# A weight-block sum of the fast-multiplication chains made by an adding transfer instead of by VectorE

## The chip, the core and the metric

The kernel runs on one core of one Trainium2 chip. The metric is the device time of the whole launch in microseconds; of the kernel before, three runs were timed. All names of lines are those of the profile: L687 is line 687 of the kernel before. TensorE is PE in the profile, VectorE DVE, ScalarE ACT, GpSimd POOL, SyncE SP.

## The reference

One layer of a diffusion trunk, on 1024 latent tokens and 256 context tokens of width 1024, all in float32. The change touches the two feed-forwards, their first two weight matrices only:

```
def swiglu(h, w1, w3, w2):
    return (jax.nn.silu(h @ w1) * (h @ w3)) @ w2
...
x = x + 0.5 * m_l[2] * swiglu(modulate(rms_norm(x, norm1_w), m_l[0], m_l[1]), ffn1_w1, ffn1_w3, ffn1_w2)
...
x = x + 0.5 * m_l[8] * swiglu(modulate(rms_norm(x, norm3_w), m_l[6], m_l[7]), ffn2_w1, ffn2_w3, ffn2_w2)
```

`w1` and `w3` are 1024 x 2816, `w2` is 2816 x 1024. Between the feed-forwards stand retention and gated linear attention; the output is the normed latent stream.

## The kernel before, in words

**Arithmetic.** Every float32 operand is split into a high part (`hi`, the value rounded to the matmul's type, made by ScalarE, L421) and a low part (`lo`, the rest, made by VectorE, L422); a product is three matmuls, hi x hi, hi x lo and lo x hi (L426 to L428).

**Chains.** Two columns of 128 of the hidden layer and two groups of 512 tokens form a 2 x 2 block product over 8 tiles of the inner dimension, and `chain` computes it with seven half products instead of eight, after Strassen and Winograd. `seven_w` prepares the seven weight tiles of a chain, each 128 x 512. It loads four blocks from DRAM (`a11`, `a21`, `a22`, `a12`) into tiles called `raw`, and makes the other three from them on VectorE: L687 `s1 = a21 + a22`, L689 `a21 = a11 - a21`, L690 `a11 = s1 - a11`, L694 `a12 = a12 - a11`. In the order of use the seven tiles are `a11`, `s1`, the new `a11`, `a12`, the new `a21`, the new `a12`, `a22`; each is split into `whi` and `wlo` and used in 12 matmuls of 512 columns. `hidden` runs one chain for `w1` (its outputs go through SiLU) and one for `w3` (multiplied into them) per pair of hidden columns: 9 pairs in the first feed-forward, 10 in the second, so 38 chains. The first columns of each feed-forward are computed the plain way by `first1` and `first2`.

**Buffers.** There are six `raw` tiles (`NR`) for the five that a chain uses and for other weights; a load of a later chain waits until an earlier tile's last reader is done. There are six `whi` and six `wlo` tiles (`NH`).

**Beside the chains.** In the first feed-forward VectorE also computes the modulation columns (`mod_sum`, L523, one per loaded `ada` tile); in both it combines the half products (L715, L743, L751) and makes the sums for `w2` (L796, L798). The loads and the stores of the results (`gd`, `sd`) all go through SyncE's one queue (L663 is the load of a `raw` tile), in which each entry waits for its own tile. GpSimd issues no transfer at all; it computes the small power step of the norms (`nr`, L1665 and, in the second half, L147), and in the context part the low parts of some weights.

**Order.** A scheduler fixes each engine's order at build time from priorities (`WPRI` lifts a chain's preparation) and its own estimates. Around the first chain VectorE's order matters: after the norm's power step (GpSimd, `nr`) it makes four diagonal tiles (`ndiag`, L590), with which TensorE spreads the norm factors over the partitions (L599).

Of the kernel before, what the change touches and what calls it, by code (L numbers as in the profile page):

```python
# [14 lines left out]
ALU = mybir.AluOpType  # L15
# [377 lines left out]
class Trunk:  # L393
# [285 lines left out]
    def seven_w(self, w, f):  # L679
        e = self.nc.vector  # L680
        with self.tc.high_priority(offset=WPRI):
            lo, hi = slice(0, 512), slice(512, 1024)
            a11, a21, a22 = (self.raw_half(w[i][:, q]) for i, q in ((f, lo), (f + 1, lo), (f + 1, hi)))
            s1 = self.raw_half()
            a12 = self.raw_half(w[f][:, hi])
            r = [self.half(a11)]
            e.tensor_tensor(out=s1, in0=a21, in1=a22, op=ALU.add)  # L687
            r.append(self.half(s1))
            e.tensor_tensor(out=a21, in0=a11, in1=a21, op=ALU.subtract)  # L689
            e.tensor_tensor(out=a11, in0=s1, in1=a11, op=ALU.subtract)  # L690
            r.append(self.half(a11))
            r.append(self.half(a12))
            r.append(self.half(a21))
            e.tensor_tensor(out=a12, in0=a12, in1=a11, op=ALU.subtract)  # L694
            r.append(self.half(a12))
            r.append(self.half(a22))
        return r
# [1701 lines left out]
```

## Time and profile before

| | |
|---|---|
| three runs | 2085.08, 2083.58, 2084.71 us; median 2084.71 |
| profiled execution | span 2087.0 us, granted clock 0.998; no other time of it is listed |
| busy share of the span | PE 99%, PEld 84%, DVE 71%, ACT 47%, POOL 10% |
| first feed-forward's chains | about 75 to 425 us and on into the stage behind |
| second feed-forward's chains | about 1440 to 1840 us |

The span runs from the first to the last instruction of one execution. Rows of the order of time give start and duration in us, engine, line, operation, what it writes and reads, and in brackets how long the engine had been idle and what ended that. A row of SPq is the issue of a transfer, not the transfer; the time from issue to landing is listed apart.

### The profile page before, as it was taken

What the parts mean: (1) busy time and instruction counts of PE and PEld (TensorE: products, weight loads), DVE (VectorE), ACT (ScalarE), POOL (GpSimd) and SP (SyncE); (2) the same over time, 40 slices, a digit from 0 to 9 for tenths busy, and PEclk for the clock granted to TensorE, in tenths of its full rate; (3) what the DMA queues carried; (4) which work ended last, traced back from release to release, by engine and by line L of the source; (5) the groups of instructions that cost most, each with busy time, mean ns of one, the idle gap of its engine ahead of it and who ended that gap; (6) DMA issues with size and microseconds to landing.
All of it is one profiled execution on the core that took longest, in us unless ns stands there. A gap on an engine that the chain in (4) does not pass through costs nothing.

```text
span 2087.0 us, 34162 instructions
## 1 busy us (share of the span) xinstructions
PE 2071.6 (99%) x12352; PEld 1763.0 (84%) x12352; DVE 1471.9 (71%) x2660; ACT 973.3 (47%) x1818; POOL 199.3 (10%) x195
## 2 busy tenths in 40 slices
PE   9999999999999999999999999999999999999998
PEld 6888888888889999998788988888888888888888
DVE  6889999666776445765577478767776666765586
ACT  5433433435544445566475246444434344344553
POOL 0000000000015665001021001000000000010000
PEclk9999999999999999999999999999999999999999
DMA  9277667449886553674233233242344444477774
GB/s 348 84 241 237 232 217 256 149 165 371 277 289 222 181 183 115 195 219 129 76 108 98 79 91 105 90 162 81 112 156 147 144 163 157 151 235 229 218 237 151
DMA packets 201082, 370.58 MB, mean 178 GB/s; under 512 B 23249, under 2 KB 35921, under 8 KB 200785
## 3 DMA queue, kind: packets, MB, share of 16 engines
q1 hardware_dynamic: 200768, 368.33, 53.7%
q8 instruction: 97, 1.59, 0.3%
q14 instruction: 73, 0.59, 0.1%
q10 hardware_dynamic: 144, 0.07, 0.0%
HBM read 292.68 MB, written 67.24 MB: 172 GB/s over the span
## 4 chain that ended last, share of the span: by engine, by line
PE 77%; DVE 10%; DMA 8%; issue 3%; ACT 1%; SPq 0%; DVEq 0%; POOLq 0%; ACTq 0%
PE psa L147 18%; PE psa L426 10%; PE psa L428 10%; PE psa L427 10%; PE psb L147 9%; PE psb L427 7%; PE psb L428 7%; PE psb L426 7%; DVE junk L523 2%; DVE wlo L422 2%; DMA raw<-in_w 2%; DMA raw<-sd 2%; DVE hl L422 1%; DMA raw<-gd 1%; DMA hl<-sd 1%
## 5 line engine op out<-in xcount | busy, mean ns | idle before, releaser
L421 ACT ACTIVATE whi<-raw 128x512 fp32r<-128x512 f32 x371 | 233.9, 631 | 502.7 <-issue 160.6
L422 DVE TENSOR_TENSOR wlo<-raw,whi 128x512 fp32r<-128x512 f32 x371 | 254.1, 687 | 178.0 <-ACT whi L421 175.6
L426 PE MATMUL psa<-hh,whi 128*128 128x512 f32 x684 | 267.0, 390 | 1.2 <-ACT s L738 0.6
L428 PE MATMUL psa<-hh,wlo 128*128 128x512 f32 x684 | 266.3, 389 | 0.0
L427 PE MATMUL psa<-hl,whi 128*128 128x512 f32 x684 | 266.2, 389 | 0.0
L427 PE MATMUL psb<-hl,whi 128*128 128x512 f32 x568 | 221.6, 390 | 0.5 <-DVE hl L422 0.3
L428 PE MATMUL psb<-hh,wlo 128*128 128x512 f32 x568 | 221.3, 390 | 0.2 <-DVE wlo L422 0.2
L426 PE MATMUL psb<-hh,whi 128*128 128x512 f32 x568 | 221.1, 389 | 0.0
L426 PEld LDWEIGHTS psa<-hh,whi 128*128 128x128 f32 x684 | 128.4, 188 | 28.9 <-ACT s L711 1.7
L147 DVE TENSOR_TENSOR wlo<-raw,whi 128x512 fp32r<-128x512 f32 (+1 forms) x140 | 88.5, 647 | 90.8 <-ACT whi L147 80.1
L147 PE MATMUL psa<-hl,whi 128*128 128x512 f32 x384 | 152.5, 397 | 0.0
L147 PE MATMUL psa<-hh,whi 128*128 128x512 f32 x384 | 152.3, 397 | 0.0
L147 PE MATMUL psa<-hh,wlo 128*128 128x512 f32 x384 | 152.2, 396 | 0.0
L428 PEld LDWEIGHTS psa<-hh,wlo 128*128 128x128 f32 x684 | 128.4, 188 | 26.6
L427 PEld LDWEIGHTS psa<-hl,whi 128*128 128x128 f32 x684 | 128.5, 188 | 26.3
L422 POOL TENSOR_TENSOR hl<-s,hh 128x512 fp32r<-128x512 f32 x88 | 132.4, 1530 | 145.2 <-DVE hl L422 81.1
L147 ACT ACTIVATE whi<-raw 128x512 fp32r<-128x512 f32 (+1 forms) x140 | 82.5, 599 | 119.7 <-PE psa L147 94.1
L427 PEld LDWEIGHTS psb<-hl,whi 128*128 128x128 f32 x568 | 106.6, 188 | 24.7 <-DVE hl L422 2.7
L428 PEld LDWEIGHTS psb<-hh,wlo 128*128 128x128 f32 x568 | 106.6, 188 | 23.1 <-DVE wlo L422 1.2
L426 PEld LDWEIGHTS psb<-hh,whi 128*128 128x128 f32 x568 | 106.6, 188 | 22.2
L428 PE MATMUL psa<-hh,hl 128*128 128x256 f32 x392 | 111.1, 284 | 0.0
L426 PE MATMUL psa<-hh,hh 128*128 128x256 f32 x392 | 111.1, 283 | 0.0
(443 smaller groups left out, 4820.4 us busy)
## 6 DMA issues: line engine op xcount, KB each, us to landing
raw<-in_w SPq DMA_DIRECT2D x242, 256.0 KB, 3.3
s<-in_w SPq DMA_DIRECT2D x198, 256.0 KB, 3.7
gd<-s SPq DMA_DIRECT2D x154, 256.0 KB, 2.8
ada<-in_adaT SPq DMA_DIRECT2D x60, 512.0 KB, 4.6
raw<-gd SPq DMA_DIRECT2D x91, 256.0 KB, 3.5
sd<-s SPq DMA_DIRECT2D x44, 256.0 KB, 2.7
raw<-sd SPq DMA_DIRECT2D x44, 256.0 KB, 3.2
hh<-in_w SPq DMA_DIRECT2D x44, 256.0 KB, 4.0
```

The lines of the kernel that those rows point to most:

```text
L147: self.rec.add(self.eng, lambda: f(*map(get, a), **{x: get(v) for x, v in k.items()}), outs, ins, name, a, k)
L421: nc.scalar.activation(hi, src, AF.Copy)
L422: (eng or nc.vector).tensor_tensor(out=lo, in0=src, in1=hi.bitcast(F32), op=ALU.subtract)
L426: mm(ps, wa[0], xa[0], start=start, stop=False, skip_group_check=more)
L427: mm(ps, wa[0], xa[1], start=False, stop=False, skip_group_check=more)
L428: return mm(ps, wa[1], xa[0], start=False, stop=stop, skip_group_check=more)
L523: nc.vector.tensor_tensor_reduce(out=self.junk, in0=t, in1=self.cs[s], scale=1.0, scalar=self.col("ada_b")[:, j:j + 1], op0=ALU.mult, op1= ...
```

## The change

In `seven_w`, `s1` is now loaded with the block `a21` by SyncE, and GpSimd then issues a transfer of the block `a22` from DRAM that adds into `s1`. `a21` and `a22` are still loaded on their own, since both are needed later. VectorE's sum L687 is gone. The order in which the five tiles are taken changes with it: `s1`, `a11`, `a21`, `a22`, `a12`. From L684 on, every line of the changed kernel has a number higher by one; the new line 685 is the adding transfer.

```
-            a11, a21, a22 = (self.raw_half(w[i][:, q]) for i, q in ((f, lo), (f + 1, lo), (f + 1, hi)))
-            s1 = self.raw_half()
+            s1 = self.raw_half(w[f + 1][:, lo])
+            a11 = self.raw_half(w[f][:, lo])
+            self.nc.gpsimd.dma_start(s1, w[f + 1][:, hi], accum_op=ALU.add)
+            a21, a22 = (self.raw_half(w[f + 1][:, q]) for q in (lo, hi))
             a12 = self.raw_half(w[f][:, hi])
             r = [self.half(a11)]
-            e.tensor_tensor(out=s1, in0=a21, in1=a22, op=ALU.add)
             r.append(self.half(s1))
             e.tensor_tensor(out=a21, in0=a11, in1=a21, op=ALU.subtract)
```

Per chain SyncE issues five loads instead of four, GpSimd one transfer instead of none. Three places show what moves.

SyncE's queue at a chain of `w3` in the second feed-forward, before. The loads into raw_3373, 3374, 3375 and 3377 are `a11`, `a21`, `a22` and `a12` (3376 is `s1`, which is not loaded); `gd1` and `sd1` are stores of results:

```order
L663 DMA raw_3373_16610<-in_w23 128x512
L797 DMA sd1<-s_3310_16284 128x512
L799 DMA sd1<-s_3311_16285 128x512
L663 DMA raw_3374_16612<-in_w23 128x512
L752 DMA gd1<-s_3303_16194 128x512
L663 DMA raw_3375_16614<-in_w23 128x512
L752 DMA gd1<-s_3304_16208 128x512
L663 DMA raw_3377_16617<-in_w23 128x512
L752 DMA gd1<-s_3338_16439 128x512
```

The same place now; raw_3373 to raw_3377 are `s1`, `a11`, `a21`, `a22` and `a12`:

```order
L663 DMA raw_3373_16631<-in_w23 128x512
L798 DMA sd1<-s_3310_16303 128x512
L800 DMA sd1<-s_3311_16304 128x512
L663 DMA raw_3374_16633<-in_w23 128x512
L753 DMA gd1<-s_3303_16213 128x512
L663 DMA raw_3375_16636<-in_w23 128x512
L753 DMA gd1<-s_3304_16227 128x512
L663 DMA raw_3376_16638<-in_w23 128x512
L753 DMA gd1<-s_3338_16459 128x512
L663 DMA raw_3377_16640<-in_w23 128x512
```

The load of `s1` stands where that of `a11` stood, that of `a11` where that of `a21` stood, and so on; the fifth comes one store later.

VectorE's order at the end of the first norm and the start of the first chain, before. raw_224, 225, 226 and 227 are `a11`, `a21`, `a22` and `s1` of that chain:

```order
L1664 TENSOR_SCALAR nr_160_687<-psb_159_682 128x4
L1191 TENSOR_TENSOR ada4_150_612<-raw_161_693,ada3_149_611 128x512
L1191 TENSOR_TENSOR ada4_150_612<-raw_162_697,ada3_149_611 128x512
L590 TENSOR_SCALAR ndiag_163_704<-ident_4_82,nr_160_687 128x128
L590 TENSOR_SCALAR ndiag_164_706<-ident_4_82,nr_160_687 128x128
L590 TENSOR_SCALAR ndiag_165_708<-ident_4_82,nr_160_687 128x128
L590 TENSOR_SCALAR ndiag_166_710<-ident_4_82,nr_160_687 128x128
L743 TENSOR_TENSOR s_158_677<-psa_100_313,s_158_677 128x512
L687 TENSOR_TENSOR raw_227_1137<-raw_225_1133,raw_226_1135 128x512
L613 SCALAR_TENSOR_TENSOR x10_129_466<-x10_129_466,mod_7_87,nrb_170_745 128x512
L613 SCALAR_TENSOR_TENSOR x11_130_468<-x11_130_468,mod_7_87,nrb_170_745 128x512
L689 TENSOR_TENSOR raw_225_1133<-raw_224_1131,raw_225_1133 128x512
```

The same place now; raw_225 is `a11`, raw_226 is `a21`, and L690 is the line that was L689:

```order
L1665 TENSOR_SCALAR nr_160_687<-psb_159_682 128x4
L1192 TENSOR_TENSOR ada4_150_612<-raw_161_693,ada3_149_611 128x512
L1192 TENSOR_TENSOR ada4_150_612<-raw_162_697,ada3_149_611 128x512
L690 TENSOR_TENSOR raw_226_1136<-raw_225_1133,raw_226_1136 128x512
L590 TENSOR_SCALAR ndiag_163_704<-ident_4_82,nr_160_687 128x128
L590 TENSOR_SCALAR ndiag_164_706<-ident_4_82,nr_160_687 128x128
L590 TENSOR_SCALAR ndiag_165_708<-ident_4_82,nr_160_687 128x128
L590 TENSOR_SCALAR ndiag_166_710<-ident_4_82,nr_160_687 128x128
L744 TENSOR_TENSOR s_158_677<-psa_100_313,s_158_677 128x512
L613 SCALAR_TENSOR_TENSOR x10_129_466<-x10_129_466,mod_7_87,nrb_170_745 128x512
```

The difference `a11 - a21` went ahead of the four `ndiag`; the sum behind them is gone.

GpSimd's queue from the start of the program, before: the constants, then the first norm's power step and later ones.

```order
L417 MEMSET pad_1_67 128x24
L417 MEMSET pad_2_75 128x64
L1665 ISA
L1665 TENSOR_TENSOR nr_160_687<-nr_160_687,mhalf_6_85 128x4
L1387 TENSOR_TENSOR lgu_1871_8644<-lge_1870_8642,lgu_1871_8644 128x8
```

The same queue now:

```order
L417 MEMSET pad_1_67 128x24
L417 MEMSET pad_2_75 128x64
L685 DMA raw_224_1131<-in_w11 128x512
L1666 ISA
L1666 TENSOR_TENSOR nr_160_687<-nr_160_687,mhalf_6_85 128x4
L685 DMA raw_254_1286<-in_w13 128x512
L685 DMA raw_283_1444<-in_w11 128x512
```

The first chain's adding transfer stands ahead of the first norm's power step, the others behind it; before the second feed-forward the first adding transfer stands ahead of the last norm's power step in the same way.

## Prediction

> **What bounds the kernel now.** I read the page's busy table first, then the table of windows for the two stages that hold chains (75 to 425 us: first feed-forward; 1440 to 1840 us: second), then who waited for whom there, then the order of time at the places where the change moves something.
>
> ```profile
> span 2087.0 us, 34162 instructions
> ...
> PE 2071.6 (99%) x12352; PEld 1763.0 (84%) x12352; DVE 1471.9 (71%) x2660; ACT 973.3 (47%) x1818; POOL 199.3 (10%) x195
> ```
> ```profile
> 75.00:425.00 350.00, 349.17 (x1532) 286.31 (x1531) 314.25 (x518) 134.11 (x237) 0.00 (x0) 1.00 0.63 210
> 1440.00:1840.00 400.00, 399.40 (x1762) 330.54 (x1761) 283.54 (x460) 164.66 (x284) 0.00 (x0) 1.00 0.41 139
> ```
> ```profile
> 200.00:300.00 100.00, 99.61 (x437) 81.32 (x436) 98.18 (x164) 39.54 (x70) 0.00 (x0) 1.00 0.70 231
> ```
> In a window's row stand its length, then the busy time of PE, PEld, DVE, ACT and POOL, then granted clock, DMA share and GB/s. TensorE is idle 0.83 us of 350 in the first stage and 0.60 of 400 in the second, at a granted clock of 1.00. VectorE, which the change relieves, is busy 314 of 350 us, 98% between 200 and 300. GpSimd does nothing in either.
>
> What TensorE waited for in 75 to 425 us, in total, times, longest:
>
> ```profile
> PE psa L426 <- ACT s L711: 0.6, 2, 0.4
> PE psb L428 <- DVE wlo L422: 0.2, 1, 0.2
> ```
> VectorE's lateness reaches TensorE in one wait of 0.2 us. Why so little shows in the splits, which VectorE (`wlo`) and ScalarE (`whi`) make of each weight tile before its product:
>
> ```profile
> 1512.07 0.63 ACT L421 ACTIVATE whi<-raw 128x512 fp32r<-128x512 f32 x1 [2.09 <-PE psb L427]
> ...
> 1514.81 0.63 ACT L421 ACTIVATE whi<-raw 128x512 fp32r<-128x512 f32 x1 [1.62 <-PE psb L427]
> ...
> 1517.51 0.63 ACT L421 ACTIVATE whi<-raw 128x512 fp32r<-128x512 f32 x1 [2.08 <-PE psb L427]
> ```
> Splits come every 2.72 us and each waits for TensorE, since the six `whi`/`wlo` buffers are full. The split of a tile starts when the product six earlier lets its buffer go, so five products of 2.72 us still stand ahead of it: 13.6 us, less about 1.3 us for the split itself. Estimate: weights are ready some 12 us early. A chain is seven products, 19.0 us. So the kernel is TensorE's stream plus its few gaps, and a cheaper VectorE can only win part of 0.83 + 0.60 = 1.4 us.
>
> **The change, part by part.** *Removed:* 38 sums on VectorE.
>
> ```profile
> L687 DVE TENSOR_TENSOR raw<-raw,raw x38: 674/684/693, 61.3 to 1824.1; 128x512 f32<-128x512 f32 x38
> ```
> 38 x 0.684 = 26 us of VectorE (12 in the first stage, whose VectorE is densest), all under matmuls: worth between 0 and 1.4 us. I take 0, since the TensorE waits above name L711 twice and a split once, none of them the sum.
>
> *Added:* per chain one more plain load of 256 KB and one accumulating transfer of 256 KB, issued by GpSimd, which waits for the plain load.
>
> ```profile
> q1 hardware_dynamic: 200768, 368.33, 53.7%
> ...
> raw<-in_w SPq DMA_DIRECT2D x242, 256.0 KB, 3.3
> ```
> 368.33 MB take 53.7% of the engines' span, 3.04 us per MB. 0.524 MB more per chain is 1.6 us in 19.0 us, 8% more share: 0.63 becomes 0.71 and 0.41 becomes 0.49. If the addition made its transfer cost twice (its target is read too), 0.75 and 0.53. The next row shows TensorE busy for 100.00 of 100 us at a share of 0.87, so the volume costs nothing.
>
> ```profile
> 500.00:600.00 100.00, 100.00 (x447) 82.95 (x446) 70.76 (x123) 52.37 (x99) 0.69 (x1) 1.00 0.87 298
> ```
> [...]
>
> *The wait for the addition.* No row shows a transfer that adds, or one issued by GpSimd. Its landing I bound by the landings of the loads of `raw` (third row), and its issue by GpSimd's largest frequent operation (fourth).
>
> ```profile
> 1502.58 0.33 SPq L663 DMA_DIRECT2D raw<-in_w  x1
> ```
> ```profile
> 1525.67 0.63 ACT L421 ACTIVATE whi<-raw 128x512 fp32r<-128x512 f32 x1 [1.61 <-issue]
> ```
> ```profile
> DMA to landing us min/median/max: 2.0/3.3/8.7
> ```
> ```profile
> L422 POOL TENSOR_TENSOR hl<-s,hh x88: 1285/1640/1806, 619.1 to 817.9; 128x512 fp32r<-128x512 f32 x88
> ```
> In SyncE's queue the plain load of `s1` takes the place of that of `a11` (the order's piece of this chain), so it goes out at about 1502.6, and ScalarE first reads the sum at 1525.67: 23.1 us. From the rows the path is 3.3 + 1.6 + 3.3 = 8.2 us, at most 8.7 + 1.8 + 8.7 = 19.2. Both fit, before the 12 us lead is touched; price 0. The load of `a11` moves to the next slot in that queue (1508.02 in the same stretch) and is wanted 14.9 us later, by the split at 1522.95:
>
> ```profile
> 1508.02 0.33 SPq L663 DMA_DIRECT2D raw<-in_w  x1
> ```
> ```profile
> 1522.95 0.63 ACT L421 ACTIVATE whi<-raw 128x512 fp32r<-128x512 f32 x1 [1.61 <-issue]
> ```
> The load of `a21` takes the place of `a22`'s; the sum that had to wait for `a22` (L687) stood in VectorE's order where L689, which waits for `a21`, stands now: 0. `a22` and `a12` go one place later, with four and more splits to spare. Behind the waiting addition GpSimd's queue holds, in the steady chains, only the next addition; behind the split of `s1` ScalarE's queue holds the chain's later splits, which is why a late sum would reach TensorE.
>
> *What moves onto the path: the first chain.* VectorE's order now has L689 (`a21 = a11 - a21`) ahead of the four `ndiag`; TensorE's `ndiag` matmuls stand in its stream at 60.34.
>
> ```profile
> 57.16 0.93 SPq L663 DMA_DIRECT2D raw<-in_w  x2
> ```
> ```profile
> raw<-in_w SPq DMA_DIRECT2D x2, 256.0 KB, 3.2
> ```
> ```profile
> 58.32 1.28 DVE L1191 TENSOR_TENSOR ada<-raw,ada 128x512 fp32r<-128x512 f32 x2
> 59.91 0.88 DVE L590 TENSOR_SCALAR ndiag<-ident,nr 128x128 f32<-128x128 f32 x4 [0.30 <-POOL nr L1665]
> 60.69 0.68 DVE L743 TENSOR_TENSOR s<-psa,s 128x512 f32<-128x512 f32 x1
> ```
> ```profile
> 60.03 0.39 PE L428 MATMUL psa<-hh,ada 128*128 128x512 f32 x1
> 60.34 1.13 PE L599 MATMUL psb<-ndiag,ones 128*128 128x128 f32 x8
> ```
> The first of the two loads at 57.16 is now `a21`. It lands 3.2 us later, at 60.4; L689 takes about 0.6, so `ndiag` starts at 61.0 instead of 59.91: 1.1 us later, of which TensorE has about 0.1 in hand. Price **+1.0 us**. With landings of 2.0 and 5.3 us (the second is this stretch's median while the queue is full, next block) `ndiag` starts at 60.2 or 63.1: between 0.2 and 3.1 us. Behind it the norm's steps follow without the two sums' time between them, so it isn't paid twice.
>
> *GpSimd's queue.* The first addition stands ahead of the norm's power step there, which VectorE and then TensorE wait for.
>
> ```profile
> 58.48 1.39 POOL L1665 TENSOR_TENSOR nr<-nr,mhalf 128x4 f32<-128x4 f32 x1 [57.56 <-DVE nr L1664]
> ```
> ```profile
> 43.56 4.34 SPq L663 DMA_DIRECT2D raw<-in_w  x6
> ```
> ```profile
> raw<-in_w SPq DMA_DIRECT2D x9, 256.0 KB, 5.3
> ```
> The `s1` load is the fifth of the six, so out by 47 us, in by about 52.3, and GpSimd then has 6 us before it is needed. In the second feed-forward the same order holds: the load goes out at 1425.86, lands by 1429.2, and the power step starts at 1437.36, 8 us later. Price 0.
>
> ```profile
> 1425.86 1.83 SPq L663 DMA_DIRECT2D raw<-in_w  x2
> ```
> ```profile
> 1437.36 1.01 POOL L147 TENSOR_TENSOR nr<-nr,mhalf 128x4 f32<-128x4 f32 x1 [44.02 <-DVE nr L147]
> ```
> *Sum:* 2087.0 + 1.0 = 2088.0 us of span. The results list no separate time of the profiled execution; its span lies 2.3 us above the median of the three runs, 2084.71, to which I add the same 1.0: **2085.7 us**, from 2084.71 + 0.2 - 1.4 = 2083.5 to 2084.71 + 3.1 = 2087.8.
>
> **The rivals.** *A small gain* (chance 0.12): the stalls in both stages go and `a21` lands early. For it speaks that VectorE is relieved where it is 98% busy, against it that it was the last to be late only for 0.2 us. 2083.5 us.
>
> *GpSimd's issue holds VectorE* (0.06; slower). The next rows show the two engines shutting each other out: one VectorE operation of 0.69 us took 1.78 us at 631.51, with GpSimd busy from 631.05.
>
> ```profile
> 631.05 1.69 POOL L422 TENSOR_TENSOR hl<-s,hh 128x512 fp32r<-128x512 f32 x1 [3.68 <-DMA xd<-x]
> ```
> ```profile
> 631.51 1.78 DVE L813 TENSOR_TENSOR hh<-hh,hl 128x512 f32<-128x512 f32 x1
> ```
> Place: 100 to 300 us, 10.5 chains, for which I take the row of 200 to 300: VectorE has 1.8 us idle in 100, so 0.34 per chain, and gains 0.60. A hold of h costs (h - 0.94) of lead per chain; 12 us of lead are gone from h = 2.1 us on. The 1.1 us seen above would cost nothing; 4 us would cost 3.06 x 10.5 - 12 = 20 us, so 2106 us. The second stage's VectorE, 71% busy, hides 4 us. [...]
>
> *The addition lands too late* (0.05; slower). [...] It needs more than 23.1 us from load to landing before a split is late, and 35 before TensorE is; each microsecond beyond would return in up to 38 chains, so 36 us give 2085.7 + 38 = 2124 us. Against it: 19.2 from the rows. [...]
>
> *The first addition is slow to issue* (0.03; slower): if GpSimd needs 11 instead of under 6 us for its first such transfer, the power step at 58.48 and TensorE behind it lose 5 us: 2090.7 us.
>
> **How the numbers follow.** The forecast has 0.72, the small gain 0.12; both lie within 0.2% (4.2 us, about what a measurement of this kernel can tell from no change). The three slower ones have 0.14 together. 0.02 stays for a gain beyond the TensorE gaps counted here, for which I know no mechanism. So faster 0.02, same 0.84, slower 0.14. The range takes forecast and small gain with their bounds, 2083.5 to 2087.8, and, since the unseen transfer is the least known, reaches down by the runs' spread below the median (1.1 us, to 2082.4) and up to 2090.0, next to the slow first issue.
>
> **What would show it.** Right: TensorE's idle time in 75 to 425 and 1440 to 1840 stays under 2 us; about 1 us of wait appears before L599 (`ndiag`) near 60 us; VectorE's busy time falls by some 26 us; no `whi` split waits for the addition's landing. Wrong: TensorE waiting for `wlo` or `whi` in the chains, VectorE operations of over 1 us there, GpSimd's issues taking several microseconds each, or ScalarE waiting on a transfer from `in_w` into `raw`.

## The result, and the profile after

The changed kernel takes 2091.54 us (median of five runs, 2090.85 to 2094.80), the kernel before 2084.71 (2083.58 to 2085.85): ratio 1.0032, 95% interval 1.0022 to 1.0043. It is slower by about 6.8 us. 2085.7 was forecast, up to 2090.0.

The page and the table of windows of the changed kernel, in the columns explained in the prediction:

```profile
span 2089.5 us, 34308 instructions
...
PE 2070.7 (99%) x12352; PEld 1763.5 (84%) x12352; DVE 1448.1 (69%) x2622; ACT 973.3 (47%) x1818; POOL 239.7 (11%) x233
```
```profile
75.00:425.00 350.00, 346.65 (x1515) 284.50 (x1514) 301.28 (x495) 133.88 (x235) 13.94 (x16) 1.00 0.72 230
1440.00:1840.00 400.00, 399.40 (x1765) 330.40 (x1764) 269.26 (x442) 162.87 (x281) 16.88 (x20) 1.00 0.54 163
```

VectorE has 23.8 us less to do. TensorE, idle for 0.83 us of the first stage before, is idle for 3.35; in the second stage nothing changed (0.60). The profiled execution of before that the prediction starts from (span 2087.0 us) was a long one: a second one of the same kernel (before_again) had a span of 2083.0, and 6.5 us is what is to be explained.

What TensorE waited for up to 450 us, in total, times, longest, in the changed kernel and then, for 60 to 425 us, in before_again:

```profile
PE psa L426 <- ACT s L712: 2.5, 2, 2.1
...
PE psb L428 <- DVE wlo L422: 0.7, 1, 0.7
PE psb L599 <- DVE ndiag L590: 0.5, 1, 0.5
```
```profile
PE psa L426 <- ACT s L711: 0.3, 1, 0.3
```

L712 (L711 before) is ScalarE's copy of a PSUM bank, and the next product of a chain into the bank waits for it: in the rows below the copy ends at 171.42 and the product starts at 171.47. The one long wait and what led to it, in the changed kernel's order of time, VectorE, ScalarE and TensorE:

```profile
158.23 0.69 DVE L690 TENSOR_TENSOR raw<-raw,raw 128x512 f32<-128x512 f32 x1 [1.86 <-issue]
...
169.07 0.68 DVE L716 TENSOR_TENSOR s<-psa,s 128x512 f32<-128x512 f32 x1
```
```profile
169.79 0.63 ACT L739 ACTIVATE s<-s 128x512 f32<-128x512 f32 x1 [1.70 <-DVE s L716]
170.33 0.61 ACT L421 ACTIVATE whi<-raw 128x512 fp32r<-128x512 f32 x1
170.85 0.57 ACT L712 COPY s<-psa 128x512 f32<-128x512 f32 x1
```
```profile
168.94 0.39 PE L428 MATMUL psa<-hh,wlo 128*128 128x512 f32 x1
171.47 0.51 PE L426 MATMUL psa<-hh,whi 128*128 128x512 f32 x1 [2.14 <-ACT s L712]
171.80 0.60 PE L427 MATMUL psa<-hl,whi 128*128 128x512 f32 x1
172.20 0.63 PE L428 MATMUL psa<-hh,wlo 128*128 128x512 f32 x1
```

L690 (`a21 = a11 - a21`) held VectorE for 1.86 us; VectorE worked without a pause from there to 171.5 and was late with L716; SiLU (L739) waited for L716 at the head of ScalarE's queue; the copy, whose product had ended at 166.6, stood behind it; TensorE waited 2.14 us. What L690 waited for is the load of `a21`. It went out at 153.42; the load for the same chain went out at 145.06 in the kernel before (second row). The table of waits puts these 1.86 us down to "issue"; the load landed at 158.15:

```profile
153.42 0.33 SPq L663 DMA_DIRECT2D raw<-in_w  x1
```
```profile
145.06 0.33 SPq L663 DMA_DIRECT2D raw<-in_w  x1
```

Such waits of VectorE in 75 to 425 us, in the changed kernel and in before_again:

```profile
DVE raw L690 <- DMA raw<-in_w: 7.4, 6, 2.0
...
DVE raw L690 <- issue: 2.9, 2, 1.9
```
```profile
DVE raw L687 <- DMA raw<-in_w: 0.2, 1, 0.2
```

So of the 12 us of sums that VectorE was spared in this feed-forward, 10.3 us went into standing still, ahead of operations that others wait for. The long stall cost more than its 2.14 us. The third column from the end of the next row says that TensorE's clock was granted at 0.60 in the 4 us from 171, and the matmuls took 0.63 instead of 0.39 us. That is 4 x 0.40 = 1.6 us of full clock lost.

```profile
171.00:175.00 4.00, 3.53 (x9) 2.81 (x10) 3.96 (x8) 1.28 (x3) 0.00 (x0) 0.60 0.59 198
```

The adding transfers themselves did what was expected of them. Issue on GpSimd, then time from issue to landing, then the two queues' packets, bytes and share:

```profile
L685 POOL DMA_DIRECT2D raw<-in_w x38: 856/874/1067, 53.2 to 1813.8; - x38
...
DMA to landing us min/median/max: 3.7/4.9/7.4
```
```profile
q1 hardware_dynamic: 206240, 378.29, 54.9%
q0 software_dynamic: 5472, 9.96, 2.9%
```

Where 6.2 of the 6.5 us lie, by matching TensorE's matmuls of the two traces one by one: 0.6 at L599 near 60 us, 5.2 in the first stage (3.0 of idle time, 1.6 of clock), 1.2 in the context's part (600 to 700 us), -2.0 between 1000 and 1440 us (before_again has a stretch at half clock there, the changed kernel none), 0.2 in the second stage, 1.0 at the end.

### The profile page after: what moved, and what is told of

Its sections match the earlier page's. It is cut to its first block, busy times and chain, and to the rows that moved or that the text cites. A ratio compares the mean times of both kernels' runs of the same rounds, so it can differ in the third digit from the quotient of the medians.

```text
span 2089.5 us, 34308 instructions
## 1 busy us (share of the span) xinstructions
PE 2070.7 (99%) x12352; PEld 1763.5 (84%) x12352; DVE 1448.1 (69%) x2622; ACT 973.3 (47%) x1818; POOL 239.7 (11%) x233
## 3 DMA queue, kind: packets, MB, share of 16 engines
q1 hardware_dynamic: 206240, 378.29, 54.9%
q0 software_dynamic: 5472, 9.96, 2.9%
## 4 chain that ended last, share of the span: by engine, by line
PE 92%; DMA 3%; DVE 3%; ACT 1%; issue 1%; SPq 0%; DVEq 0%; POOLq 0%; ACTq 0%
PE psa L147 18%; PE psa L426 12%; PE psa L427 12%; PE psa L428 12%; PE psb L427 9%; PE psb L428 9%; PE psb L426 9%; PE psb L147 8%; DMA raw<-in_w 1%; DMA hl<-sd 1%; PE psa L1205 1%; DVE wlo L422 0%; DVE hl L422 0%; ACT whi L421 0%; DVE nt L147 0%
## 5 line engine op out<-in xcount | busy, mean ns | idle before, releaser
L422 DVE TENSOR_TENSOR wlo<-raw,whi 128x512 fp32r<-128x512 f32 x371 | 254.5, 687 | 152.5 <-ACT whi L421 151.5
L426 PE MATMUL psa<-hh,whi 128*128 128x512 f32 x684 | 267.7, 391 | 3.2 <-ACT s L712 2.5
L428 PE MATMUL psa<-hh,wlo 128*128 128x512 f32 x684 | 266.9, 390 | 0.0
L428 PE MATMUL psb<-hh,wlo 128*128 128x512 f32 x568 | 221.2, 389 | 0.7 <-DVE wlo L422 0.7
L426 PE MATMUL psb<-hh,whi 128*128 128x512 f32 x568 | 221.1, 389 | 0.2 <-ACT hh L421 0.2
L426 PEld LDWEIGHTS psa<-hh,whi 128*128 128x128 f32 x684 | 128.8, 188 | 31.7 <-ACT s L712 4.2
L422 POOL TENSOR_TENSOR hl<-s,hh 128x512 fp32r<-128x512 f32 x88 | 138.4, 1600 | 139.8 <-DVE hl L422 82.0
L428 PEld LDWEIGHTS psa<-hh,wlo 128*128 128x128 f32 x684 | 128.8, 188 | 26.8
L428 PEld LDWEIGHTS psb<-hh,wlo 128*128 128x128 f32 x568 | 106.6, 188 | 23.4 <-DVE wlo L422 1.4
L426 PEld LDWEIGHTS psb<-hh,whi 128*128 128x128 f32 x568 | 106.6, 188 | 22.7 <-ACT hh L421 0.6
L685 POOL DMA_DIRECT2D raw<-in_w x38 | 33.5, 882 | 788.0 <-DVE wlo L422 196.0
L428 PE MATMUL psa<-hh,hl 128*128 128x256 f32 x392 | 111.1, 284 | 0.0
```

What stands on the lines that cost most here:

```text
L422: (eng or nc.vector).tensor_tensor(out=lo, in0=src, in1=hi.bitcast(F32), op=ALU.subtract)
L426: mm(ps, wa[0], xa[0], start=start, stop=False, skip_group_check=more)
L428: return mm(ps, wa[1], xa[0], start=False, stop=stop, skip_group_check=more)
L685: self.nc.gpsimd.dma_start(s1, w[f + 1][:, hi], accum_op=ALU.add)
```

## The experiments

**Theory A**: the new order of loads makes `a21` late, VectorE's queue stands at L690, and in the first stage that reaches TensorE through ScalarE's copy. **Rival B**: the adding transfer itself costs, in each of 38 chains. **Rival C**: the scheduler, for which the adding transfer is a GpSimd operation without a landing, made a bad order (in the first four expectations C is wider: any accident of order, at 171 us above all). Each ratio is to runs of the kernel before made beside that kernel's. TensorE's idle time is the window's length less PE's busy time; the last column adds VectorE's waits for loads into `raw`, L690 and its like ("issue" rows included).

| kernel | us | ratio to before [95%] | TensorE idle 75-425 | VectorE waits there |
|---|---|---|---|---|
| the change | 2091.54 | 1.0032 [1.0022, 1.0043] | 3.35 | 10.3 |
| before_again | 2085.63 | 1.0000 [0.9991, 1.0009] | 0.33 | 0.2 |
| ff1_only | 2089.30 | 1.0020 [1.0011, 1.0029] | 4.71 | 5.2 |
| ff2_only | 2084.99 | 0.9999 [0.9990, 1.0008] | 0.27 | 0.6 |
| late_s1 | 2104.36 | 1.0088 [1.0074, 1.0103] | 7.23 | 8.7 |
| dve_sum | 2097.79 | 1.0054 [1.0035, 1.0072] | 8.77 | 9.6 |
| planned | 2090.48 | 1.0024 [1.0014, 1.0034] | 4.41 | 10.0 |
| own_tile | 2096.56 | 1.0050 [1.0035, 1.0065] | 4.87 | 6.5 |
| ns18_before | 2086.19 | 1.0000 [0.9991, 1.0010] | 0.54 | 0.2 |
| seven_raw | 2090.97 | 1.0024 [1.0015, 1.0033] | 6.44 | 11.2 |
| seven_raw_before | 2080.55 | 0.9973 [0.9963, 0.9983] | 0.76 | 0 |
| no_a21 | 2089.80 | 1.0015 [1.0006, 1.0023] | 1.92 | 0 |
| pool_loads | 2089.90 | 1.0022 [1.0013, 1.0031] | 1.69 | 4.7 |
| late_sub | 2089.55 | 1.0016 [1.0007, 1.0026] | 1.97 | 2.5 |
| late_sub_before | 2086.30 | 1.0006 [0.9998, 1.0015] | 1.92 | 0.3 |
| use_order | 2096.85 | 1.0052 [1.0040, 1.0064] | 4.65 | 8.9 |
| seven_late_sub | 2084.87 | 0.9991 [0.9982, 1.0000] | 0.18 | 5.0 |
| triple_sum | 2087.82 | 1.0016 [1.0008, 1.0025] | 1.75 | 0 |
| t2_four | 2082.64 | 0.9985 [0.9976, 0.9994] | 0.00 | 0.2 |

### Which feed-forward, and is it the addition?

before_again is the kernel before, unchanged.

> The kernel before, unchanged, for a profile of an execution at its usual time: the profiled span of 2087.0 us stands 4.3 us above what the median of 2084.71 us leaves for a span if the 2.0 us between time and span in the runs of the changed kernel hold for this one too. Expected ratio 0.999 to 1.001, span 2082 to 2084 us, and no stretch near 1025 us at half the granted clock; with the span of 2089.5 us for the changed kernel the loss to be explained is then 6 to 7 us and not 2.5.

Its span is 2083.0 us, as expected; but the stretch at half clock near 1025 us (0.50 for 3.4 us in the first execution) is there too, with a granted clock of 0.998 in both, so it isn't what made the first execution long.

ff1_only and ff2_only keep the old lines in the other feed-forward:

```
+            if self.ff == 1:        # ff2_only: self.ff == 2
                 s1 = self.raw_half(w[f + 1][:, lo])
...
+            else:
+                a11, a21, a22 = (self.raw_half(w[i][:, q]) for i, q in ((f, lo), (f + 1, lo), (f + 1, hi)))
```

> The change in the first feed-forward alone. Theory A (the s1 load takes a raw slot first, the load of a21 goes out some 8 us later, and L690 holds VectorE 1 to 2 us at a time, which costs only where VectorE is dense, in 75 to 425 us): 2090 to 2093 us, all of the loss. Rival B (the adding transfers themselves cost, by their doubled engine time or by GpSimd's issues, in each of the 38 chains): 18 of 38 chains, 2087 to 2089 us. Rival C (one accident of order near 171 us with the clock drop behind it): all of the loss here as well, and 4 us of it between 160 and 176 us.

> The change in the second feed-forward alone. Theory A: 2084 to 2086 us, no loss, since VectorE has slack there (L690 waits for a21 there too, 9.5 us in all, but TensorE's idle time in 1440 to 1840 us did not grow). Rival B: 20 of 38 chains, 2087 to 2089 us. Rival C: 2084 to 2086 us.

The first stage of ff1_only and the second of ff2_only:

```profile
75.00:425.00 350.00, 345.29 (x1510) 283.45 (x1509) 300.93 (x493) 133.60 (x235) 13.90 (x16) 1.00 0.71 230
```
```profile
1440.00:1840.00 400.00, 399.40 (x1763) 330.39 (x1762) 269.29 (x439) 164.33 (x285) 15.68 (x18) 1.00 0.52 165
```

The change in the second feed-forward is free: 20 adding transfers, TensorE idle for 0.60 us as before. In the first it costs 3.5 us (2.3 to 6.0 by the interval), just under A's range; this interval and that of the whole change (4.6 to 9.0) overlap. In its trace TensorE falls 6.2 us behind before_again within the first stage, as against 5.2 in the change, and gets 2.3 back between 425 and 1040 us, where nothing was changed. Its longest wait, 2.86 us, lies at 212 us and not at 171, so one accident of order at 171 us isn't the cause. Rival B would have put half of the loss into ff2_only.

dve_sum has the five loads of the change in their order, and VectorE adds:

```
             a11 = self.raw_half(w[f][:, lo])
-            self.nc.gpsimd.dma_start(s1, w[f + 1][:, hi], accum_op=ALU.add)
             a21, a22 = (self.raw_half(w[f + 1][:, q]) for q in (lo, hi))
             a12 = self.raw_half(w[f][:, hi])
             r = [self.half(a11)]
+            e.tensor_tensor(out=s1, in0=s1, in1=a22, op=ALU.add)
```

> The loads of the changed kernel in their order (s1, a11, a21, a22, a12, so five a chain), but VectorE adds the block a22 to s1, and no transfer adds. Theory A (s1 takes one of the six raw tiles from its first load on, so the load of a21 goes out late and VectorE's queue stands at L690): the tiles are taken as in the changed kernel, so L690 waits as there, and VectorE has its 38 sums back as well: 2090 to 2096 us. Theory C (the scheduler's order, for which an adding transfer is a GpSimd operation of some 1.5 us without a landing, puts work of VectorE in a worse order): no such operation stands in it, 2084 to 2087 us. Rival B (the adding transfer's own cost): gone, 2084 to 2087 us.

```profile
75.00:425.00 350.00, 341.23 (x1495) 279.34 (x1494) 307.36 (x505) 131.68 (x233) 0.00 (x0) 1.00 0.65 217
```

With no adding transfer at all the loss is larger, 1.0054, above A's range: TensorE is idle for 8.77 us. So five loads in this order can lose as much with no addition in a transfer, and B falls as the only cause; C with it, as far as it rests on the transfer's price. But it isn't the loss of the change over again. VectorE's sum now waits for the late load of `a22` as well (6.1 of the 9.6 us of its waits), and 4.8 us of TensorE's idle time are waits for a `wlo`, not for the copy.

planned gives the scheduler the transfer's measured price:

```
+        if eng == "POOL" and name == "dma_start":
+            cost, bytes = 0.9, 4 * size * outs[0].shape[0]
...
-        op.port = eng == "POOL" or name in SHARED and not any(self.psum(v.root) for v in ins)
+        op.port = eng == "POOL" and name != "dma_start" or name in SHARED and not any(self.psum(v.root) for v in ins)
...
+                elif o.name == "dma_start":
+                    o.end = s + c + 5.0
```

> The change as it is, but the scheduler that fixes the orders counts the adding transfer with 0.9 us of issue, without VectorE being shut out, and with a landing 5 us later, as measured, instead of as a GpSimd operation of 1.5 us without a landing. Theory C (the order made under the wrong price costs): 2084 to 2087 us. Theory A (six raw tiles, and the load of a21 third in SyncE's queue, whatever the price of the addition): L690 still waits for a21 in 75 to 425 us, 2088 to 2093 us.

VectorE waited for `a21` for 10.0 us as in the change, the time is 1.0024. C falls in this form: the right price doesn't make the order better.

### Why is the load of a21 late?

late_s1 loads `a11` and `a21` first:

```
+            a11, a21 = self.raw_half(w[f][:, lo]), self.raw_half(w[f + 1][:, lo])
             s1 = self.raw_half(w[f + 1][:, lo])
-            a11 = self.raw_half(w[f][:, lo])
             self.nc.gpsimd.dma_start(s1, w[f + 1][:, hi], accum_op=ALU.add)
-            a21, a22 = (self.raw_half(w[f + 1][:, q]) for q in (lo, hi))
+            a22 = self.raw_half(w[f + 1][:, hi])
```

> The change in both feed-forwards with the loads in the order a11, a21, s1 and its addition, a22, a12, so that a11 and a21 get their tiles first, as before. Theory A: L690 no longer waits for a21, the addition still lands ahead of the split of s1, and the time is that of before within 2 us (2083 to 2087 us). Rival B: the same 38 adding transfers, so 2090 to 2093 us. Rival C: another order of the instructions, so the 4 us at 171 us go or come by chance; no wait of L690 would have to go with it.

A miss, and the largest loss of all. L690 waited for 2.3 us only, though no wait was expected, but the addition came late; the first row is ScalarE's, the second VectorE's at `a11 = s1 - a11`, 75 to 425 us:

```profile
ACT whi L421 <- DMA raw<-in_w: 31.0, 10, 5.0
```
```profile
DVE raw L691 <- DMA raw<-in_w: 6.4, 6, 1.4
```

In nine of the 17 chains up to 425 us the split of `s1` started 0.1 us after the addition had landed, which was 8.9 to 12.3 us after the plain load had gone out. Load and addition one after the other take that long, and this order leaves no room for it; the order of the change leaves it and delays `a21`.

own_tile gives `s1` a tile of its own, with 18 instead of 19 tiles called `s`; ns18_before is its control (the kernel before with `NS = 18`).

```
-            s1 = self.raw_half(w[f + 1][:, lo])
+            s1 = self.tile(self.fp, [P, 512], F32, "s1w")
+            self.nc.sync.dma_start(s1, w[f + 1][:, lo])
```

> The change, but s1 has a tile of its own, and the six raw tiles serve the other four blocks; for the room, the tiles called s are 18 instead of 19. To be compared with the kernel before at 18, not 19 (ns18_before). Theory A: the loads of a11 and a21 go out earlier than before, L690 waits nowhere, ratio to ns18_before 0.999 to 1.001. Theory C: the scheduler still misjudges the transfer, 2 to 6 us over ns18_before. Rival B: 3 to 6 us over it.

> Control for own_tile: the kernel before with 18 tiles called s instead of 19. All theories: 2084 to 2092 us; the tiles called s hold half products and wait for their combination, so one fewer may cost a few us; what it costs is not the change's.

The control is the kernel before (1.0000). own_tile is at 1.0050, of which 4.2 us are one wait at L599, behind a wait of 3.4 us for a load in VectorE's queue there; TensorE's clock then stood at half for 6.8 us, which cost 3.4 us more (granted clock 0.997 over the span, 0.998 in before_again). It settles nothing: the single tile's load stood in SyncE's queue until the tile was free, and the load of `a21` was late behind it.

seven_raw has seven `raw` tiles instead (and 18 `s`, 4 `t2`); seven_raw_before is the kernel before with the same three numbers.

```
-NT2 = 5
+NT2 = 4
...
-NR = 6
+NR = 7
```

> The change with seven raw tiles instead of six; for the room, 18 tiles called s instead of 19 and 4 instead of 5 called t2 (in the stage of the context). To be compared with seven_raw_before. Theory A (s1 takes one of six raw tiles from its first load on, and the later loads of the chain wait for the next tile): with a seventh the load of a21 goes out as early as before, L690's waits for it in 75 to 425 us fall from 10 us to under 3, and the ratio to seven_raw_before is 0.999 to 1.001. If the fifth load or its place in SyncE's queue costs, whatever the tiles: 3 to 7 us over seven_raw_before.

> Control for seven_raw: the kernel before with seven raw tiles, 18 called s and 4 called t2. All theories: 2083 to 2088 us; the seventh tile has nothing to win where TensorE is idle for 0.3 us in 350.

VectorE's waits in seven_raw:

```profile
DVE raw L690 <- DMA raw<-in_w: 8.5, 7, 3.0
...
DVE raw L690 <- issue: 2.7, 1, 2.7
```

The number of tiles is not it: the waits stayed, and against its control the change now costs 1.0024 / 0.9973 = 1.0051 (1.0032 to 1.0070 from the ends of the two intervals). That part of theory A falls.

no_a21 leaves the load of `a21` out:

```
-            a21, a22 = (self.raw_half(w[f + 1][:, q]) for q in (lo, hi))
+            a21, a22 = self.raw_half(), self.raw_half(w[f + 1][:, hi])
...
-            e.tensor_tensor(out=a21, in0=a11, in1=a21, op=ALU.subtract)
+            e.tensor_tensor(out=a21, in0=a11, in1=s1, op=ALU.subtract)
```

> The change with the load of a21 left out and the difference made from s1 in its place (so the weights of that product are not the reference's): 38 adding transfers, but four plain loads a chain as before, and a tile for a21 only when it is written. Theory A: L690 has no load to wait for and five loads have become four: 2083 to 2087 us. Rival B (the adding transfer's own cost: its doubled engine time, GpSimd's issues): 2089 to 2093 us.

No wait for a load is left, and TensorE's idle time falls from 3.35 to 1.92 us; 1.0015 remain, above A's range and within B's. pool_loads leaves all loads in and takes that of `s1` out of SyncE's queue:

```
-            s1 = self.raw_half(w[f + 1][:, lo])
+            s1 = self.raw_half()
+            self.nc.gpsimd.dma_start(s1, w[f + 1][:, lo])
```

> The change, but GpSimd issues both transfers into s1, the plain one and the adding one, so SyncE's queue has its four loads a chain in the order a11, a21, a22, a12 as before; six raw tiles. If the queue is what makes a21 late (s1's load ahead of it, waiting for its own tile): L690's waits in 75 to 425 us fall from 10 us to under 3, 2084 to 2087 us. If s1's hold on one of six tiles is what does it after all: the waits stay, 2089 to 2094 us.

The waits fell by half (4.7 us, not under 3), TensorE's idle time in the first stage to 1.69: the place in SyncE's queue is part of it. The total didn't fall (1.0022), for another reason: TensorE lost 3.0 us once in the second stage, where ScalarE's queue stood for 5.7 us at L533, whose load was late (2.3 us in before_again, 2.6 in the change; why it was later here isn't shown):

```profile
1687.00 0.63 ACT L533 ACTIVATE row<-row 128x512 f32<-128x512 f32 x1 [5.74 <-DMA row<-in_c]
...
1688.58 0.56 ACT L713 COPY s<-psa 128x512 f32<-128x512 f32 x1
```
```profile
PE psa L426 <- ACT s L713: 3.0, 1, 3.0
```

It is the same last step again: the copy (L713 there) behind something late in ScalarE's queue.

### Is it VectorE's wait that reaches TensorE?

late_sub writes `s1 - a11` into the tile of `s1`, so the difference with `a21` can come two products later; late_sub_before is the same in the kernel before. use_order loads `a12` ahead of `a21` and `a22` as well. seven_late_sub is late_sub with the tiles of seven_raw.

```
-            e.tensor_tensor(out=a21, in0=a11, in1=a21, op=ALU.subtract)
-            e.tensor_tensor(out=a11, in0=s1, in1=a11, op=ALU.subtract)
-            r.append(self.half(a11))
+            e.tensor_tensor(out=s1, in0=s1, in1=a11, op=ALU.subtract)
+            r.append(self.half(s1))
             r.append(self.half(a12))
+            e.tensor_tensor(out=a21, in0=a11, in1=a21, op=ALU.subtract)
             r.append(self.half(a21))
```

> The change, but the new a11 (s1 - a11) is written into the tile of s1 after the split of s1, so the difference of a11 and a21 (L690 in the changed kernel) need not stand ahead of it and comes right before its own split, two products later. Theory A in the form that L690's wait in VectorE's queue is what costs: no VectorE operation waits for a21, 2083 to 2087 us. If the late loads themselves cost (raw tiles too few, whatever stands in VectorE's queue): 2089 to 2093 us. Rival B: 2089 to 2093 us.

> Control for late_sub: the kernel before (sum by VectorE, four loads a chain) with the same move of the difference of a11 and a21 behind the split of the new a11. All theories: 2083 to 2087 us if the move itself is worth nothing; late_sub minus this one is then what the adding transfer with its extra load still costs once VectorE doesn't wait for a21 early.

> As late_sub (the difference with a21 comes two products later), and a12 is loaded ahead of a21 and a22, in the order of use. Theory A: no VectorE operation waits for a21, a12 is early for its split; 2085 to 2089 us, at or under late_sub's 2089.6. If the number of raw tiles is what costs, in whatever order they are filled: 2089 to 2093 us.

> late_sub with seven raw tiles (18 called s, 4 called t2): the difference with a21 two products later, and a tile more. Theory A: no operation waits for a load in 75 to 425 us; ratio to seven_raw_before 0.999 to 1.001, 2083 to 2087 us; not faster than before by more than 1 us, since TensorE's idle time in both stages is 1 us in all. If the fifth load costs whatever the tiles: 2087 to 2091 us.

late_sub brings the waits from 10.3 to 2.5 us, the stall at 171 us from 2.14 to 0.18 (a wait of 1.5 us is left at 287) and the loss to 1.0016, still over the 2083 to 2087 of A and within the ranges of the other two. Its control is at 1.0006 and has as much TensorE idle time in the first stage, 1.92 us against 1.97: once the difference stands later, the change adds no idle time there. seven_late_sub has no stall left in the first stage (first row seven_raw, second seven_late_sub):

```profile
75.00:425.00 350.00, 343.56 (x1502) 281.98 (x1501) 298.39 (x491) 132.39 (x234) 13.91 (x16) 1.00 0.71 230
```
```profile
75.00:425.00 350.00, 349.82 (x1535) 287.35 (x1535) 306.00 (x503) 133.47 (x238) 13.91 (x16) 1.00 0.71 234
```
```profile
DVE raw L693 <- DMA raw<-in_w: 5.0, 4, 2.3
```

So with seven tiles the move of one VectorE operation takes TensorE's idle time there from 6.44 us (seven_raw) to 0.18 and the whole from 2090.97 to 2084.87 us, though the loads are the same five and VectorE still waits 5.0 us for them: a wait costs by where it stands. Against seven_raw_before it is 0.9991 / 0.9973 = 1.0018 (0.9999 to 1.0037 in the same way), which is not told apart from the ratio expected. use_order is a miss: `a21` now lands still later, VectorE waits 8.9 us for it at the later place, and that place isn't free either (1.0052, TensorE idle 4.65 us).

triple_sum leaves the loads as before and has VectorE make the sum three times:

```
-            e.tensor_tensor(out=s1, in0=a21, in1=a22, op=ALU.add)
+            for _ in range(3):
+                e.tensor_tensor(out=s1, in0=a21, in1=a22, op=ALU.add)
```

> The kernel before with the sum of two weight blocks made three times over by VectorE (the same result each time), 1.37 us of VectorE more a chain at that place and nothing else added; no transfer changes. Theory A (a microsecond or two of VectorE ahead of the weight differences and the combination of half products reaches TensorE, through the ScalarE copy of a PSUM bank that stands behind them in ScalarE's queue, and the 12 us lead of the split weights doesn't cover that): TensorE waits for L711 in 75 to 425 us, 2087 to 2094 us. The prediction's reasoning (12 us of lead cover it; the first stage has 35 us of VectorE idle and the sums add 25): 2084 to 2087 us.

TensorE's idle time in the first stage goes from 0.33 to 1.75 us, in two waits for L712, and the time to 1.0016, at the lower end of A's range: VectorE's time there isn't covered, with no transfer changed.

t2_four is the kernel before with one tile fewer in the context's stage.

> The kernel before with 4 instead of 5 tiles called t2, and nothing else of seven_raw_before. In that run's trace the 4 us that it gained came between 1000 and 1440 us and none in the chains. If t2 is the cause: 2080 to 2082 us. If the seventh raw tile is (weights of the stages in between go through the raw tiles too): 2084 to 2087 us.

At 0.9985 it has more than half of seven_raw_before's gain, and in both traces TensorE is about 4 us ahead by 1440 us and not at all by 900: the gain is another stage's. seven_raw_before, at 2080.55 us, is faster than both kernels of this case, without the change.

## Why the prediction was wrong, step by step

**The step that failed** is "the sum that had to wait for `a22` (L687) stood in VectorE's order where L689, which waits for `a21`, stands now: 0", and behind it the cover of 12 us that every wait was measured against. L690 waited 10.3 us where L687 had waited 0.2. The exchange of places itself was nearly as the prediction has it: counted in TensorE's matmuls, so that the lag between the traces drops out, the load of `a21` landed on average 0.5 us later than that of `a22` in before_again (16 chains of 75 to 425 us, from 2.7 us earlier to 4.5 later), and VectorE came to L690 1.2 us earlier than to L687. What the step left out is the spare of that wait. In before_again VectorE came to L687 a median of 1.7 us after the landing, in two of the 16 chains before it; in the chain of the stall at 171 us it came 0.4 us after, and the load landed 2.7 us later. The prediction checked `a11` against ScalarE's split, but `a21` by its place alone.

And the 12 us are the lead of the split weights, read from rows at 1512 us in the second feed-forward. In the first it isn't there everywhere: the prediction's row `PE psb L428 <- DVE wlo L422` is a split that came 0.2 us late. Above all TensorE has a second supplier, the copy of the bank, and that has hardly any lead. In before_again, at another chain:

```profile
282.25 0.63 ACT L738 ACTIVATE s<-s 128x512 f32<-128x512 f32 x1 [3.58 <-DVE s L715]
282.79 0.61 ACT L421 ACTIVATE whi<-raw 128x512 fp32r<-128x512 f32 x1
283.31 0.56 ACT L711 COPY s<-psa 128x512 f32<-128x512 f32 x1
```
```profile
283.92 0.50 PE L426 MATMUL psa<-hh,whi 128*128 128x512 f32 x1 [0.32 <-ACT s L711]
```

It is the sequence of the stall in the kernel before: SiLU waits for VectorE's L715, the copy stands behind it, and TensorE already waits 0.32 us for the copy. Pairing each copy of before_again with the next matmul that waits for ScalarE, 16 of 65 in 75 to 425 us end under 0.5 us ahead of it (six of them 0.05 us, and these are what let the matmul go), while the least of the 76 in 1440 to 1840 us is 1.50. This fits that the same waits of VectorE (9.5 us of L690 there, none over 1.4, the row below) cost nothing in the second feed-forward.

```profile
DVE raw L690 <- DMA raw<-in_w: 9.5, 9, 1.4
```

The row that named it stood in the prediction: `PE psa L426 <- ACT s L711`, twice, the longest 0.4 us. It was read as part of the 1.4 us that could at best be won, and was the place where most of VectorE's lateness arrives: 2.5 us in the change, against 0.7 at a split.

**The first chain**: +1.0 us (0.2 to 3.1) was forecast, 0.5 is there. `a21` was a little earlier:

```profile
59.68 0.69 DVE L690 TENSOR_TENSOR raw<-raw,raw 128x512 f32<-128x512 f32 x1 [0.29 <-DMA raw<-in_w]
60.28 0.87 DVE L590 TENSOR_SCALAR ndiag<-ident,nr 128x128 f32<-128x128 f32 x4
```
```profile
60.71 1.13 PE L599 MATMUL psb<-ndiag,ones 128*128 128x128 f32 x8 [0.53 <-DVE ndiag L590]
```

**Volume**: right. The DMA share is 0.72 and 0.54; a megabyte of the adding transfers took 2.9% / 9.96 = 0.29% of the engines' span, one of the plain ones 54.9% / 378.29 = 0.145%, so a megabyte that is added cost twice as much here.

**The wait for the addition**: right in the change's own order. 8.2 us (at most 19.2) were estimated from the load's issue to the landing; it is 7.9 to 13.3 in the first feed-forward and 7.2 to 10.5 in the second, and ScalarE's split came some 6 us or more after each landing. late_s1 shows that it was not so far from the end.

**GpSimd's issue** took 0.87 us, and VectorE's operations beside it their usual time (a split 0.69 us, as elsewhere): that rival is out. So are the slow first issue (1.07 us, its power step at 58.28 instead of 58.48) and the late addition.

**What stays open**: VectorE's waits for loads come with the fifth load (0.2 us with four, in before_again) and depend on SyncE's order (pool_loads), but no order tried with five loads was free of it in the first feed-forward. With no waits for loads at all (no_a21), 0.0015 remain; late_sub_before shows that a mere change of VectorE's order can cost 1.6 us of TensorE's idle time in this stage, so part of the rest may be that, but it was not told apart from a small cost of the adding transfers there. The 1.2 us in the context's part were not followed up; kernels without the change move by nearly as much there (triple_sum comes 0.9 us nearer to before_again).

## What to carry to other kernels

Before a wait is priced at nothing, list every supplier of the bound engine and take each one's own lead: here the weights had some 12 us in the stage looked at, and the PSUM copy under 0.5 in a quarter of the cases of the other. When an operation becomes a transfer, look at which load the operations that stay behind now wait for, and what is queued behind them; read how much spare that wait has now, and not only its place; the volume and the issue were the harmless part. The longest of the bound engine's few remaining waits, however short, names the path on which the next disturbance will arrive.

## What the runs showed of the hardware

TensorE's clock fell to half with waits of some 2 us in the middle of the program: with the 2.14 us in the change to 0.50 for 3.4 us (171.8 to 175.2 us), so that this wait cost 3.7; with 2.86 us in ff1_only, where the first stage has 345.29 / 1510 = 0.2287 us of busy time per matmul, as against 346.65 / 1515 = 0.2288 in the change and 349.67 / 1538 = 0.2274 in before_again; and in late_s1, whose longest wait for a copy there is 2.0 us, to 0.77 on average in the 4 us from 171 and 0.99 over the first stage. With the 4.2 us in own_tile it stood at half for 6.8 us. With 3.0 us in pool_loads it did not fall: the second stage has 396.41 / 1748 = 0.2268 us per matmul, the kernel before 399.40 / 1762 = 0.2267. So a wait of 2.14 us brought the fall and one of 3.0 did not; what decides between them was not shown.

An adding transfer of 256 KB from DRAM into SBUF landed, in the changed kernel, in 3.7 to 7.4 us beside other traffic, median 4.9, plain loads into the same tiles in a median of 3.5.
